# A mixer and feed-forward stack: the first chunks of a feed-forward split during the mixer before it, into tiles that its last down pairs use again

## The chip, the cores and the metric

The kernel runs on one core of a Trainium2 chip. The metric is the device time of one execution in microseconds (us), as the median of several runs; the profile is taken from one more execution of the same program.

## The reference

The input x is 256 tokens by 1024 features in float32. A first block (mixer, cross attention to a memory, mixture of experts) is not touched by the change. Then come two layers of this, each with its own weights:

```python
for l in range(2):
    x = layer_norm(alpha * x + 0.5 * swiglu(x, ffn_w_gu[l, 0], ffn_w_down[l, 0]), ...)
    mix = token_mixers(x, w_in[l], sink[l], ..., diff_subln[l], w_out[l], l)
    x = layer_norm(alpha * x + mix, ...)
    x = layer_norm(alpha * x + 0.5 * swiglu(x, ffn_w_gu[l, 1], ffn_w_down[l, 1]), ...)
```

`swiglu` is silu(x Wg) * (x Wu), times Wd, with 2816 hidden features. `token_mixers` has four attentions of four heads each (window with a sink, latent, axial, differential), whose outputs are joined and projected by `w_out`. `layer_norm` subtracts the mean, multiplies by 1/sqrt(var + eps) and by a gain, and adds a bias.

## The kernel before

Tokens lie in two tiles of 128 (t = 0, 1). Every product is made of three float32r matmuls (`mm3`, L310 to L312): the high part of one side by the high part of the other, high by low, and low by high. ACT copies the high part (`wh` of a weight, L279; `xh` of an activation, L391), and the low part is what is left after subtraction, on DVE (L392 for `xl`, L283 for `wl`).

Weights come from memory in 1 MB chunks of 128 x 2048, in the order in which they are used, by SP into a ring of four buffers (`raw`, L260); SP waits for a buffer that is free. `weight` (L265) splits a chunk into two pairs of high and low parts, 128 x 1024 each, into a ring of tiles (`wh`, `wl`, four each), or into tiles of its own (`own`, L291). The low part goes to DVE, or to POOL where `on_pool` says so: `plan` (L300) writes there, for the next chunks, whether POOL makes the low part and after which of the norm's powers it is issued.

The program is two times feed-forward, mixer, feed-forward (loop in `build`). The instructions of an engine are issued in an order that a scheduler of the framework sets from the program's dependences; `pe_order` keeps PE's order as written, and `issue_after` adds an edge of order alone.

- `ffn` (L1270): `first` takes chunks 0 and 1 (`NAT` = 2) with x as the stationary side, so that t = 0 can go ahead before x of t = 1 is there: for each t 48 matmuls of 256 columns. Then `up` chunks and `down` pairs alternate, and the last three down pairs (`TAIL` = 3) come from `own` tiles, so that the accumulators of t = 0 are finished first and its norm runs beside the matmuls of t = 1.
- `mixer2` (L1354): `mixer2_state` (L1395) makes the tiles that live through the mixer, loads and scales the sink (L1408, L1409) and `sub`, the gain of the differential attention's norm (L1415: 128 KB in pieces of 256 B; L1416: POOL multiplies it), then come projections and attentions, and at the end the output projection `dense_sq` (L341) with `ln_part` as its end. Behind it `plan("--1-")` sends the four low parts of the next feed-forward's chunks 0 and 1 to POOL, the third behind the power of t = 1.
- the norm: `ln_state` (L1241) has POOL scale the residual (`xa` = alpha x, L1247); `ln_part` (L1253) adds the product (L1261) and takes statistics (L1262); `layer_norm` (L1225) merges them (L1229), has POOL raise the variance to -1/2 (`rsqrt`, pow at L418), and makes in two halves of 512 columns (x - mean) * gain (L1234) and times 1/std plus bias (L1235, `x`). PE transposes each half (L401), ACT and DVE split it.

I call the passage from a mixer to a feed-forward seam B and the one from a feed-forward to a mixer seam A. There are two of each.

Of the kernel before, what the change touches and what calls it, by code (L numbers as in the profile page):

```python
# [12 lines left out]
AF = mybir.ActivationFunctionType  # L13
# [185 lines left out]
class Net:  # L199
    def __init__(s, ctx, tc, a, out):  # L200
        s.tc, s.nc, s.a, s.out = tc, tc.nc, a, out
        s.pos = 0
        s.on_pool = [None, None]
        s.pows, s.ahead = [], []
        s.dense_tags = ["a", "b"]
        s.nw, s.pool_mod = 0, 4
        pool = lambda n, b, **k: ctx.enter_context(tc.tile_pool(name=n, bufs=b, **k))
        s.const = pool("const", 1)
        s.ring = pool("ring", 4)
        s.xp = pool("xp", 1)  # L210
        s.st = pool("st", 4)
        s.psum = pool("psum", 1, space=bass.MemoryType.PSUM)
        nc = s.nc
        s.ident = s.const.tile([128, 128], F32, name="ident")
        s.mhalf = s.const.tile([128, 8], F32, name="mhalf")
        nc.vector.memset(s.mhalf, -0.5)
# [48 lines left out]
    def weight(s, width=CH, parts=2, pool=None, own=None, cuts=1):  # L265
# [4 lines left out]
        for i in range(parts):  # L270
# [12 lines left out]
            i = eng.tensor_tensor(l[:, :n], rc, h[:, :n].bitcast(F32), op=OP.subtract)  # L283
            if eng is s.nc.gpsimd:
                s.pool_lo = i
            if after:
# [954 lines left out]
    def ln_state(s, p, x, li):  # L1241

        g, b = s.norm_weights(p, li)
        xa = []
        for t in range(NT):
            xa.append(p.tile([128, D], F32, name=f"xa{t}"))
            i = s.nc.gpsimd.tensor_scalar(xa[t], x[t], ALPHA, None, op0=OP.mult)  # L1247
            if li == 0:
                s.issue_after(i, s.pool_lo)
        st = [s.st.tile([128, 2 + 2 * t, 6], F32, name="lnst", tag=f"lnst{t}", bufs=2) for t in range(NT)]  # L1250
        return g, b, xa, st
# [18 lines left out]
    def ffn(s, x, hs, li, last):  # L1270
        nc = s.nc
        with ExitStack() as ctx:
            p = s.pool(ctx, "ffn")
            acc = s.banks()
            hf = {}
# [24 lines left out]
            def first():  # L1300

                ps = [s.bank("mm") for _ in range(NT)]
                ws = [s.weight(cuts=1 if li else 2) for _ in range(NAT)]
                for i in range(NAT):
# [32 lines left out]
            nx = None if last else s.xsplit()  # L1337
            w = [s.weight(own=s.own(p, i)) for i in range(TAIL)]
            norm = lambda t: [s.ln_part(p, x, ln, 0.5, t, c, acc[t][c], nx) for c in range(2)]
# [10 lines left out]
            norm(1)  # L1350
            s.on_pool = []
        return nx

    def mixer2(s, x, hs, l):  # L1354
# [28 lines left out]
        with ExitStack() as ctx:  # L1383
            s.dense_tags = ["a", "b"]
            p = s.pool(ctx, "mix2o")
            ln = s.ln_state(p, x, 3 * l + 1)
            nx = s.xsplit()
            s.dense_sq(o, lambda t, c, ps: s.ln_part(p, x, ln, 1.0, t, c, ps, nx))
            s.plan("--1-")
        return nx  # L1390

    def pair(s, p, name, *shape):
        return [p.tile([128] + list(shape), F32R, name=f"{name}{i}") for i in range(2)]

    def mixer2_state(s, p, l):  # L1395

        nc = s.nc
        m = {}
        for n in ("wk", "ck"):
            m[n] = s.pair(p, n, S)  # L1400
        for n in ("wv", "cv", "mv", "dv"):
            m[n] = p.tile([128, NT, 128 if n in ("wv", "cv") else 256], F32, name=n)
        for n in ("wq", "cq", "dq", "dk"):
            m[n] = s.pair(p, n, 2, S)
        for n in ("mq", "mk"):
            m[n] = [p.tile([96, 4, S], F32R, name=f"{n}{i}") for i in range(2)]
        m["far"], m["qscale"] = s.far, s.qscale
        sink = s.bcast(p, "win_sink_2", 4, 4 * l)  # L1408
        nc.gpsimd.tensor_scalar(sink, sink, -1.0, None, op0=OP.mult)  # L1409
        m["sink"] = sink  # L1410
        lam_init = 0.8 - 0.6 * math.exp(-0.3 * l)
# [254 lines left out]
```

## Time and profile before

| what | value |
|---|---|
| median of 3 runs | 1740.98 us (1739.96 to 1743.69) |
| profiled execution: its own time | 1743.4 us |
| its span in the trace | 1741.7 us |
| mean granted TensorE clock | 0.937 |
| PE busy | 1576.9 us, 91% of the span |
| DVE busy | 840.0 us, 48% |
| ACT busy | 656.5 us, 38% |
| POOL busy | 286.5 us, 16% |
| low parts on POOL (L283) | 42, 2463 ns each |
| low parts on DVE (L283) | 314, 1249 ns each |

The engines' shares are means over stages with different limits. The mixture of experts, in the first half, waits for weights from memory; the six stages behind it fill the span from about 840 us on, and there PE is close to always busy. A wait is given with the line that waits and the instruction that ended it. The clock is the TensorE clock that was granted, as a share of 2.4 GHz.

### The profile page before, as it was taken

The page shows a single profiled execution, that of the slowest core. Times are in us where ns is not written, and L with a number is a line of the kernel's source. Part 1 is how long each engine was busy: PE and PEld are TensorE (multiplying, and loading weights), DVE is VectorE, ACT ScalarE, POOL GpSimd, SP SyncE. Part 2 cuts the span into 40 slices and gives each one's busy share as a digit, 9 for nine tenths or more (in the row PEclk, how much of TensorE's full clock was granted, in tenths as well). Part 3 has the DMA queues.
Part 4 walks back from the last instruction along what each step waited for, and adds up shares of the span by engine and source line. Part 5 has one row for each costly group of instructions (what it writes and reads, how often), then busy time and mean ns, then how long its engine had stood idle before and what let it go on. Part 6 is the DMA issues. An engine that isn't in the chain of part 4 may idle for free.

```text
span 1741.7 us, 24950 instructions
## 1 busy us (share of the span) xinstructions
PE 1576.9 (91%) x10070; PEld 1215.4 (70%) x10070; DVE 840.0 (48%) x1468; ACT 656.5 (38%) x1125; POOL 286.5 (16%) x253
## 2 busy tenths in 40 slices
PE   8998998777776776999999989999999999989998
PEld 6777774322211221799988769999999988779997
DVE  5658653000000000554577775557654677765555
ACT  4655441000000000444545645444444536734442
POOL 4224312100000000312233250000100041330000
PEclk9999998987878886999999989999999999989999
DMA  7454959999999999855543235556455634145551
GB/s 278 149 185 142 359 192 422 417 421 421 420 421 421 421 420 421 318 194 192 195 171 135 79 145 194 184 180 241 148 191 193 243 105 147 50 179 190 179 190 72
DMA packets 66187, 419.07 MB, mean 241 GB/s; under 512 B 10641, under 2 KB 12177, under 8 KB 18705
## 3 DMA queue, kind: packets, MB, share of 16 engines
q1 hardware_dynamic: 66064, 417.39, 63.2%
q8 instruction: 82, 1.34, 0.3%
q14 instruction: 41, 0.33, 0.1%
HBM read 416.32 MB, written 1.05 MB: 240 GB/s over the span
## 4 chain that ended last, share of the span: by engine, by line
PE 63%; DMA 25%; DVE 4%; issue 4%; POOL 3%; ACT 1%; SPq 0%; DVEq 0%; POOLq 0%; ACTq 0%
DMA mraw<-in_wm 23%; PE ps L310 20%; PE ps L312 19%; PE ps L311 19%; PE ps L401 2%; PE ps L480 1%; POOL wl L283 1%; DMA raw<-in_wd 1%; DVE wl L283 1%; POOL rq L418 1%; DVE xa L1234 1%; ACT wh L279 0%; DMA bc_ln_g<-in_ln_g 0%; DVE xl L392 0%; PE ps L991 0%
## 5 line engine op out<-in xcount | busy, mean ns | idle before, releaser
L283 DVE TENSOR_TENSOR wl<-raw,wh 128x1024 fp32r<-128x1024 f32 (+2 forms) x314 | 388.9, 1249 | 292.3 <-ACT wh L279 289.4
L279 ACT ACTIVATE wh<-raw 128x1024 fp32r<-128x1024 f32 (+2 forms) x356 | 370.9, 1052 | 347.3 <-PE ps L311 177.5
L310 PE MATMUL ps<-xh,wh 128*128 128x256 f32 x1424 | 402.1, 282 | 3.4 <-ACT cv L1534 3.4
L312 PE MATMUL ps<-xh,wl 128*128 128x256 f32 x1424 | 401.3, 282 | 0.0
L311 PE MATMUL ps<-xl,wh 128*128 128x256 f32 x1424 | 401.1, 282 | 0.0
L310 PEld LDWEIGHTS ps<-xh,wh 128*128 128x128 f32 x1424 | 268.3, 188 | 7.0 <-ACT cv L1534 3.8
L311 PEld LDWEIGHTS ps<-xl,wh 128*128 128x128 f32 x1424 | 268.4, 188 | 1.8 <-issue 0.4
L312 PEld LDWEIGHTS ps<-xh,wl 128*128 128x128 f32 x1424 | 268.4, 188 | 0.8
L991 PE MATMUL ps<-mraw,xg 128*32 128x512 f32 x1024 | 168.2, 763 | 70.8 <-DMA mraw<-in_wm 70.6
L312 PE MATMUL ps<-wh,xl 128*128 128x512 f32 (+3 forms) x520 | 190.2, 370 | 6.5 <-DVE xl L392 6.3
L310 PE MATMUL ps<-wh,xh 128*128 128x512 f32 (+3 forms) x520 | 190.7, 376 | 4.7 <-ACT xh L391 3.8
L311 PE MATMUL ps<-wl,xh 128*128 128x512 f32 (+3 forms) x520 | 191.9, 370 | 2.2 <-POOL wl L283 1.1
L991 PEld LDWEIGHTS ps<-mraw,xg 128*32 128x32 f32 x1024 | 26.5, 119 | 200.4 <-DMA mraw<-in_wm 164.4
L418 POOL TENSOR_TENSOR rq<-rv,mhalf 128x1 f32<-128x1 f32 (+4 forms) x46 | 46.8, 1017 | 724.6 <-DVE rv L416 721.8
L283 POOL TENSOR_TENSOR wl<-raw,wh 128x1024 fp32r<-128x1024 f32 x42 | 103.2, 2463 | 279.5 <-ACT wh L279 180.4
L997 DVE TENSOR_TENSOR mf<-ps,mf 128x512 f32<-128x512 f32 x8 | 5.5, 692 | 238.7 <-PE ps L991 234.7
L312 PEld LDWEIGHTS ps<-wh,xl 128*128 128x128 f32 x520 | 100.8, 194 | 23.3 <-DVE xl L392 10.4
L310 PEld LDWEIGHTS ps<-wh,xh 128*128 128x128 f32 x520 | 101.0, 195 | 22.1 <-ACT xh L391 7.5
L311 PEld LDWEIGHTS ps<-wl,xh 128*128 128x128 f32 x520 | 101.4, 195 | 17.9 <-POOL wl L283 3.2
L312 PE MATMUL ps<-wh,hf 128*128 128x512 f32 x256 | 100.1, 391 | 0.0
L311 PE MATMUL ps<-wl,hf 128*128 128x512 f32 x256 | 100.1, 391 | 0.0
L310 PE MATMUL ps<-wh,hf 128*128 128x512 f32 x256 | 98.2, 390 | 0.0
(351 smaller groups left out, 1965.2 us busy)
## 6 DMA issues: line engine op xcount, KB each, us to landing
mraw<-in_wm SPq DMA_DIRECT2D x191, 1024.0 KB, 19.8
raw<-in_wd SPq DMA_DIRECT2D x179, 1024.0 KB, 4.9
raw<-in_wd SPq DMA_DIRECT2D x8, 512.0 KB, 11.0
raw<-in_wd SPq DMA_DIRECT2D x4, 832.0 KB, 4.4
bc_ln_g<-in_ln_g SPq DMA_DIRECT2D x6, 512.0 KB, 5.9
bc_ln_b<-in_ln_b SPq DMA_DIRECT2D x6, 512.0 KB, 6.6
raw<-in_wd SPq DMA_DIRECT2D x4, 768.0 KB, 4.4
bias<-in_bias SPq DMA_DIRECT2D x4, 512.0 KB, 6.5
```

The costliest lines, as they stand in the source:

```text
L279: s.nc.scalar.activation(h[:, :n], rc, AF.Copy)
L283: i = eng.tensor_tensor(l[:, :n], rc, h[:, :n].bitcast(F32), op=OP.subtract)
L310: mm(out, lhsT=lh, rhs=rh, start=start, stop=False)
L311: mm(out, lhsT=lh, rhs=rl, start=False, stop=False)
L312: mm(out, lhsT=ll, rhs=rh, start=False, stop=stop)
L401: s.nc.tensor.transpose(ps[:, b * 128:b * 128 + 128], src[:, b * 128:b * 128 + 128], s.ident)
L418: s.last_pow = s.nc.gpsimd.tensor_tensor(q, r, s.mhalf[:, :n], op=OP.pow)
L480: s.nc.tensor.matmul(out, lhsT=v(j), rhs=pt[:, 2 * i + j], start=first and j == 0, stop=last and j == 1)
L991: nc.tensor.matmul(ps[32 * e:32 * e + 32], lhsT=xg[:, k, 32 * e:32 * e + 32], rhs=w[:, e * FF:e * FF + FF], start=k == 0, stop=k == NK - 1 ...
L997: nc.vector.tensor_tensor(f, gu[1], f, op=OP.mult)
L1234: nc.vector.scalar_tensor_tensor(z[:, cs], z[:, cs], mv[:, 0:1], g[:, cs], op0=OP.subtract, op1=OP.mult)
```

## The change

The names of the new file are used here; its lines stand one or a few beside those of the old one (L284 for L283, L417 for L418, L1233 and L1234 for L1234 and L1235, L1425 and L1426 for L1415 and L1416).

- A pool `front` of eight tiles (32 KB of a partition), on the right-hand side of memory, holds the split parts of chunks 0 and 1 of a feed-forward. After a mixer it is opened by `ffn_ahead`, which `dense_sq` calls before the second half of its matmuls; `first` then uses these parts. The last down pairs 0 and 1 of the same feed-forward reuse the tiles.
- `plan("--1-")` is gone, so that the low parts of chunks 0 and 1 are made by DVE.
- The residual is scaled by ACT at the feed-forwards' norms, by POOL only at the mixers'.
- `mixer2_state` makes `wk`, `wq` and the sink first, and `sub` as before behind the other tiles.

```diff
--- before.py
+++ after.py
@@ -203,6 +203,7 @@
         s.on_pool = [None, None]
         s.pows, s.ahead = [], []
         s.dense_tags = ["a", "b"]
+        s.front, s.front_parts = None, None
         s.nw, s.pool_mod = 0, 4
         pool = lambda n, b, **k: ctx.enter_context(tc.tile_pool(name=n, bufs=b, **k))
         s.const = pool("const", 1)
@@ -281,8 +282,6 @@
             after = s.on_pool.pop(0) if s.on_pool else False
             eng = s.nc.gpsimd if after is not False or (s.pool_mod and s.nw % s.pool_mod == 0) else s.nc.vector
             i = eng.tensor_tensor(l[:, :n], rc, h[:, :n].bitcast(F32), op=OP.subtract)
-            if eng is s.nc.gpsimd:
-                s.pool_lo = i
             if after:
                 s.issue_after(i, after)
             out.append((h, l))
@@ -1244,9 +1243,10 @@
         xa = []
         for t in range(NT):
             xa.append(p.tile([128, D], F32, name=f"xa{t}"))
-            i = s.nc.gpsimd.tensor_scalar(xa[t], x[t], ALPHA, None, op0=OP.mult)
-            if li == 0:
-                s.issue_after(i, s.pool_lo)
+            if li % 3 == 1:
+                s.nc.gpsimd.tensor_scalar(xa[t], x[t], ALPHA, None, op0=OP.mult)
+            else:
+                s.nc.scalar.activation(xa[t], x[t], AF.Copy, scale=ALPHA)
         st = [s.st.tile([128, 2 + 2 * t, 6], F32, name="lnst", tag=f"lnst{t}", bufs=2) for t in range(NT)]
         return g, b, xa, st
 
@@ -1271,6 +1271,10 @@
         nc = s.nc
         with ExitStack() as ctx:
             p = s.pool(ctx, "ffn")
+            if s.front is None:
+                s.front_ctx = ExitStack()
+                s.front = s.pool(s.front_ctx, "front", side="right")
+            ctx.push(s.front_ctx)
             acc = s.banks()
             hf = {}
 
@@ -1300,7 +1304,8 @@
             def first():
 
                 ps = [s.bank("mm") for _ in range(NT)]
-                ws = [s.weight(cuts=1 if li else 2) for _ in range(NAT)]
+                ws = s.front_parts or [s.weight(cuts=1 if li else 2) for _ in range(NAT)]
+                s.front_parts = None
                 for i in range(NAT):
                     hf[i] = [p.tile([128, S], F32R, name=f"hf{u}", tag=f"hf{u}", bufs=10) for u in range(2)]
                 for t in range(NT):
@@ -1335,7 +1340,7 @@
                     for c in range(2):
                         down(t, c, i, w)
             nx = None if last else s.xsplit()
-            w = [s.weight(own=s.own(p, i)) for i in range(TAIL)]
+            w = [s.weight(own=s.own(s.front if i < NAT else p, i)) for i in range(TAIL)]
             norm = lambda t: [s.ln_part(p, x, ln, 0.5, t, c, acc[t][c], nx) for c in range(2)]
             whole, lo, hi = slice(0, 512), slice(0, 256), slice(256, 512)
             with s.pe_order():
@@ -1349,6 +1354,7 @@
                             norm(0)
             norm(1)
             s.on_pool = []
+            s.front = None
         return nx
 
     def mixer2(s, x, hs, l):
@@ -1385,9 +1391,14 @@
             p = s.pool(ctx, "mix2o")
             ln = s.ln_state(p, x, 3 * l + 1)
             nx = s.xsplit()
-            s.dense_sq(o, lambda t, c, ps: s.ln_part(p, x, ln, 1.0, t, c, ps, nx))
-            s.plan("--1-")
+            s.dense_sq(o, lambda t, c, ps: s.ln_part(p, x, ln, 1.0, t, c, ps, nx), ahead=s.ffn_ahead)
         return nx
+
+    def ffn_ahead(s):
+
+        s.front_ctx = ExitStack()
+        s.front = s.pool(s.front_ctx, "front", side="right")
+        s.front_parts = [s.weight(own=s.own(s.front, i)) for i in range(NAT)]
 
     def pair(s, p, name, *shape):
         return [p.tile([128] + list(shape), F32R, name=f"{name}{i}") for i in range(2)]
@@ -1396,18 +1407,17 @@
 
         nc = s.nc
         m = {}
-        for n in ("wk", "ck"):
-            m[n] = s.pair(p, n, S)
+        m["wk"], m["wq"] = s.pair(p, "wk", S), s.pair(p, "wq", 2, S)
+        sink = m["sink"] = s.bcast(p, "win_sink_2", 4, 4 * l)
+        nc.gpsimd.tensor_scalar(sink, sink, -1.0, None, op0=OP.mult)
         for n in ("wv", "cv", "mv", "dv"):
             m[n] = p.tile([128, NT, 128 if n in ("wv", "cv") else 256], F32, name=n)
-        for n in ("wq", "cq", "dq", "dk"):
+        m["ck"] = s.pair(p, "ck", S)
+        for n in ("cq", "dq", "dk"):
             m[n] = s.pair(p, n, 2, S)
         for n in ("mq", "mk"):
             m[n] = [p.tile([96, 4, S], F32R, name=f"{n}{i}") for i in range(2)]
         m["far"], m["qscale"] = s.far, s.qscale
-        sink = s.bcast(p, "win_sink_2", 4, 4 * l)
-        nc.gpsimd.tensor_scalar(sink, sink, -1.0, None, op0=OP.mult)
-        m["sink"] = sink
         lam_init = 0.8 - 0.6 * math.exp(-0.3 * l)
         m["nlam"] = s.nlam[l]
         sub = p.tile([128, 4, 64], F32, name="sub")
```

How the order of the instructions moves is shown at three places. POOL at the first seam A, before; `own` and `wl` are the last low parts of the feed-forward, `rq` the powers (of x for t = 0 and t = 1, 128x1; of the mixer's latent norm, 128x2):

```order
L283 TENSOR_TENSOR own<-raw,own 128x1024
L283 TENSOR_TENSOR wl<-raw,wh 128x1024
L418 TENSOR_TENSOR rq<-rv,mhalf 128x1 x2
L1409 TENSOR_SCALAR bc_win_sink_6868<-bc_win_sink_6868 128x4
L418 TENSOR_TENSOR rq<-rv,mhalf 128x2
L1416 TENSOR_SCALAR sub<-sub 128x256
L1515 TENSOR_SCALAR bc_ax_q_norm_7001<-bc_ax_q_norm_7001 128x64
```

and in the changed kernel:

```order
L284 TENSOR_TENSOR own<-raw,own 128x1024
L284 TENSOR_TENSOR wl<-raw,wh 128x1024
L417 TENSOR_TENSOR rq<-rv,mhalf 128x1
L1412 TENSOR_SCALAR bc_win_sink_6856<-bc_win_sink_6856 128x4
L1426 TENSOR_SCALAR sub<-sub 128x256
L417 TENSOR_TENSOR rq<-rv,mhalf 128x1
L417 TENSOR_TENSOR rq<-rv,mhalf 128x2
L1525 TENSOR_SCALAR bc_ax_q_norm_7005<-bc_ax_q_norm_7005 128x64
```

The scaling of `sub` has moved ahead of the second power of 128x1.

SP at the same place, with the semaphores that it waits for (PE_49 counts PE's instructions), before:

```order
L260 DMA raw<-in_wd 128x1280 [waits DMAHW4_49,DVE_49]
L260 DMA raw<-in_wd 128x2048 [waits DMAHW5_49,DVE_49]
L238 DMA bc_win_sink_6868<-in_win_sink 128x4
L1415 DMA sub<-in_diff_subln 128x4x64
L1362 DMA rope<-in_rope 128x384 [waits PE_49]
L238 DMA bc_mla_q_norm_6879<-in_mla_q_norm 128x256
```

and in the changed kernel:

```order
L261 DMA raw<-in_wd 128x1280 [waits DMAHW4_49,DVE_49]
L261 DMA raw<-in_wd 128x2048 [waits DMAHW5_49,DVE_49]
L239 DMA bc_win_sink_6856<-in_win_sink 128x4
L1425 DMA sub<-in_diff_subln 128x4x64 [waits PE_49]
L1368 DMA rope<-in_rope 128x384 [waits PE_49]
L239 DMA bc_mla_q_norm_6883<-in_mla_q_norm 128x256
```

The copy of `sub` has got a wait for PE, as that of `rope` had.

DVE at the first seam B, before, from the accumulation of t = 0 (`xa_8131`; `xa_8133` is t = 1) to its x:

```order
L1261 SCALAR_TENSOR_TENSOR xa_8131<-ps,xa_8131 128x512 x2
L1262 BN_STATS lnst<-xa_8131 128x6 x2
L1229 BN_AGGR lnmv<-lnst 128x2
L416 TENSOR_SCALAR rv<-lnmv 128x1
L1234 SCALAR_TENSOR_TENSOR xa_8131<-xa_8131,lnmv,bc_ln_g_8127 128x512 x2
L1261 SCALAR_TENSOR_TENSOR xa_8133<-ps,xa_8133 128x256 x2
L1262 BN_STATS lnst<-xa_8133 128x6 x2
L1261 SCALAR_TENSOR_TENSOR xa_8133<-ps,xa_8133 128x256 x2
L1262 BN_STATS lnst<-xa_8133 128x6
L1235 SCALAR_TENSOR_TENSOR x<-xa_8131,rq,bc_ln_b_8129 128x512 x2
L1262 BN_STATS lnst<-xa_8133 128x6
L1229 BN_AGGR lnmv<-lnst 128x2
```

and in the changed kernel (`xa_8135` and `xa_8137`), from the fourth low part of the chunks 0 and 1 on, which stands behind three more of them and the accumulation of t = 0, to the gain pass of t = 0 (L1233):

```order
L284 TENSOR_TENSOR own<-raw,own 128x1024
L1262 BN_STATS lnst<-xa_8135 128x6 x2
L284 TENSOR_TENSOR wl<-raw,wh 128x1024
L1261 SCALAR_TENSOR_TENSOR xa_8137<-ps,xa_8137 128x256 x2
L284 TENSOR_TENSOR wl<-raw,wh 128x1024
L1228 BN_AGGR lnmv<-lnst 128x2
L284 TENSOR_TENSOR wl<-raw,wh 128x1024
L1261 SCALAR_TENSOR_TENSOR xa_8137<-ps,xa_8137 128x256 x2
L1262 BN_STATS lnst<-xa_8137 128x6 x2
L284 TENSOR_TENSOR wl<-raw,wh 128x1024
L415 TENSOR_SCALAR rv<-lnmv 128x1
L1233 SCALAR_TENSOR_TENSOR xa_8135<-xa_8135,lnmv,bc_ln_g_8131 128x512 x2
```

Eight low parts of 128x1024 (four `own`, four `wl` of the two chunks behind them) now stand ahead of the gain pass of t = 0; before there was none.

## Rows read from the trace of the kernel before

**Rows 1.** The list of PE's waits from 840 us to the end (total us, times, longest).

```profile
PE ps L401 <- DVE x L1235: 7.4, 2, 3.7
PE ps L312 <- DVE xl L392: 5.7, 2, 2.9
```

**Rows 2.** PE's timeline at the first seam B (start, us, line, operation, idle before).

```profile
1026.76 1.94 PE L401 MATMUL ps<-ident,x 128*128 128x128 f32 x8 [3.68 <-DVE x L1235]
1028.53 0.58 PE L310 MATMUL ps<-wh,xh 128*128 128x256 f32 x1
...
1035.04 0.39 PE L312 MATMUL ps<-wh,xl 128*128 128x256 f32 x1 [2.85 <-DVE xl L392]
```

**Rows 3.** DVE's timeline at the first seam B.

```profile
1008.58 3.62 DVE L283 TENSOR_TENSOR wl<-raw,wh 128x1024 fp32r<-128x1024 f32 x3 [0.42 <-ACT wh L279]
...
1017.51 0.69 DVE L1261 SCALAR_TENSOR_TENSOR xa<-ps,xa 128x512 f32<-128x512 f32 x1 [2.03 <-PE ps L312]
1018.12 1.28 DVE L1262 BATCH_NORM_STATS2 lnst<-xa 128x6 f32<-128x512 f32 x2
...
1019.75 3.56 DVE L1234 SCALAR_TENSOR_TENSOR xa<-xa,lnmv,bc_ln_g 128x512 f32<-128x512 f32 x2
1023.23 0.74 DVE L1261 SCALAR_TENSOR_TENSOR xa<-ps,xa 128x256 f32<-128x256 f32 x2
...
1029.12 5.26 DVE L1234 SCALAR_TENSOR_TENSOR xa<-xa,lnmv,bc_ln_g 128x512 f32<-128x512 f32 x2
1034.30 0.68 DVE L392 TENSOR_TENSOR xl<-ps,xh 128x512 fp32r<-128x512 f32 x1
```

**Rows 4.** DVE's timeline at the first seam A.

```profile
902.02 1.40 DVE L1234 SCALAR_TENSOR_TENSOR xa<-xa,lnmv,bc_ln_g 128x512 f32<-128x512 f32 x2
903.35 1.41 DVE L1235 SCALAR_TENSOR_TENSOR x<-xa,rq,bc_ln_b 128x512 f32<-128x512 f32 x2
```

**Rows 5.** POOL's timeline at the first seam B.

```profile
1020.05 2.70 POOL L283 TENSOR_TENSOR wl<-raw,wh 128x1024 fp32r<-128x1024 f32 x1 [13.25 <-ACT wh L279]
...
1028.70 5.13 POOL L283 TENSOR_TENSOR wl<-raw,wh 128x1024 fp32r<-128x1024 f32 x2
```

**Rows 6.** Stretches: PE, PEld, DVE, ACT, POOL busy; PEclk, DMA, GB/s.

```profile
1026.00:1028.00 2.00, 1.25 (x6) 1.28 (x7) 1.93 (x5) 0.12 (x1) 0.06 (x1) 0.50 0.45 98
1030.00:1032.00 2.00, 2.00 (x11) 1.89 (x9) 2.00 (x2) 0.00 (x0) 2.00 (x2) 0.50 1.01 412
1036.00:1038.00 2.00, 2.00 (x12) 2.00 (x11) 0.49 (x1) 0.00 (x0) 2.00 (x2) 0.50 0.96 406
1040.00:1042.00 2.00, 2.00 (x19) 2.00 (x18) 1.29 (x2) 1.97 (x3) 0.00 (x0) 1.00 0.00 0
```

**Rows 7.** PE's timeline at the first seam A.

```profile
904.52 1.03 PE L401 MATMUL ps<-ident,x 128*128 128x128 f32 x8
```

**Rows 8.** POOL's timeline at the first seam A.

```profile
902.19 0.98 POOL L418 TENSOR_TENSOR rq<-rv,mhalf 128x1 f32<-128x1 f32 x1 [8.30 <-DVE rv L416]
...
907.35 0.88 POOL L1416 TENSOR_SCALAR sub<-sub 128x256 f32<-128x256 f32 x1
```

**Rows 9.** SP's timeline at the first seam A (issues).

```profile
886.05 0.43 SPq L1415 DMA_DIRECT2D sub<-in_diff_subln  x1
899.72 0.34 SPq L1362 DMA_DIRECT2D rope<-in_rope  x1
```

**Rows 10.** DMA issues from 880 to 912 us (KB, us to landing).

```profile
sub<-in_diff_subln SPq DMA_DIRECT2D x1, 128.0 KB, 8.9
```

**Rows 11.** Stretches of 2 us at the first seam A, columns as above.

```profile
890.00:892.00 2.00, 2.00 (x11) 1.65 (x10) 1.02 (x2) 0.00 (x0) 0.00 (x0) 1.00 0.08 22
892.00:894.00 2.00, 2.00 (x11) 1.65 (x10) 1.93 (x5) 0.00 (x0) 1.00 (x1) 1.00 0.07 19
```

**Rows 12.** ACT's timeline at the first seam B.

```profile
1013.28 0.38 ACT L391 ACTIVATE xh<-ps 128x256 fp32r<-128x256 f32 x1 [1.20 <-PE ps L480]
1018.91 1.06 ACT L279 ACTIVATE wh<-raw 128x1024 fp32r<-128x1024 f32 x1 [5.24 <-PE ps L312]
```

## Prediction

> **What bounds the kernel now.** I read the table of engines first: PE is busy 91% of the span, so outside the MoE in the middle, which waits for its weights from memory, a change is worth what it adds to or takes from PE's waits and its clock. The list of PE's waits after 840 us then says which waits there are to gain: at the top stand two for the norm's output x and two for the low part xl, 7.4 and 5.7 us in all, two times each [rows 1]. They are the two seams from a mixer to a feed-forward (I call them B). PE's timeline shows the first: the out-projection ends at 1026.76 - 3.68 = 1023.08, PE waits 3.68 us for x, transposes it, does a few matmuls of the first chunk and waits 2.85 us more for xl until 1035.04 [rows 2]. DVE's timeline says why: the two passes that multiply by the gain take 3.56 us for t = 0 and 5.26 us for t = 1 [rows 3], where the same two passes take 1.40 us at the seam before the mixer [rows 4]. What differs is POOL, which runs its low parts over them: at 1020.05 and at 1028.70, 2.6 us each [rows 5]. The clock view adds that PE runs at half its rate (granted 0.50, the 1.2 GHz level) after the first wait and again after the second, and is back at 2.4 GHz by 1040 [rows 6].
>
> The other seam, from a feed-forward to a mixer (A), has no wait of that size in the list. PE transposes x of t = 1 at 904.52 directly behind its own work, all eight blocks in 1.03 us [rows 7], so whatever comes late there becomes a new wait. DVE wrote that x from 903.35 on [rows 4], and could do so because POOL had given the power for t = 1 at 902.19, 0.98 us long; the scaling of sub ran only at 907.35 [rows 8]. SP had issued the copy of sub at 886.05, long before, while the copy of rope waited for PE until 899.72 [rows 9].
>
> **Seam A, which the change touches without naming it.** Two orders move. The tile of sub now lies where a feed-forward's last tiles are, so its copy waits for PE, as rope's does, three matmuls earlier: 899.72 less three times 0.11 us (19 records in 2.00 us at 1040 [rows 6]) is 899.4. And on POOL the scaling of sub now stands ahead of the power for t = 1, where it stood behind two more powers. So a pow that was ready at 902.2 is queued behind a transfer. Behind the waiting POOL stand that pow, the pow of the mixer's latent norm and the axial gains; DVE's x of t = 1 waits for the first of them, and PE for that.
>
> When does sub land? The copy took 8.9 us [rows 10], but the first four of them beside weights. From 890 on it moved alone, at 22 and 19 GB/s [rows 11]: 128 KB (131,072 B) at 20.5 GB/s are 6.4 us. I take this, since in the changed kernel no weight is ahead of it; the ends are 4.9 us (from 890 to its landing at 886.05 + 8.9) and the 8.9 us of the row. It lands at 899.4 + 6.4 = 905.8. Then 0.88 for the scaling, 0.98 for the pow [rows 8], 0.18 until DVE starts (903.17 to 903.35 before) and 0.70 for half of x [rows 4]: 908.5, instead of 904.5. With 0.1 for the hop to PE the wait is **4.1 us** (2.6 to 6.6 by the ends).
>
> A wait of that length has a second price. After the wait of 3.68 us PE ran at half rate from 1026.76 to about 1032 [rows 2, 6], some 5.2 us, of which half is lost: 2.6 us. I charge **2.6** here, with 0 and 3.4 as ends (no fall; and a stretch as long as that, plus the second one's 1.7). The latent norm's pow and the copies behind sub on SP's queue follow the same delay, and by the time x of t = 1 is multiplied they are mostly there: **0.4** (0 to 1). Seam A: +7.1 each (3 to 11).
>
> The Trainium skill, "DMA: Bandwidth & Descriptors", section "Anatomy of one DMA — SWDGE (gpsimd) path", fits a copy as about 2.0 us plus its bytes over 436,000 per us, which for sub would be an estimate of 2.3 us. The 8.9 us of this trace disagree with it; by the fit seam A would cost nothing, as the second rival says.
>
> **Seam B, which the change is about.** It takes the four low parts of chunks 0 and 1 from POOL, which frees the gain passes of DVE: 3.56 to 1.40 and 5.26 to 1.40, 6.0 us less on DVE. But those four low parts stand on DVE now, and with them the four of the next two chunks, which DVE had behind the norm, and the order puts all eight ahead of the gain pass of t = 0. One low part takes 3.62 / 3 = 1.2 us [rows 3]. DVE can start when the last split of the attention is done, at 1013.28 + 0.38, and the first high part is copied, 1.06 later [rows 12]: 1014.7. From there to the first half of x of t = 0 its work is 8 x 1.2 = 9.6, two accumulations of 0.69 (1.4), statistics 1.3, four accumulations of t = 1 (2 x 0.74 = 1.5) and their statistics, about the same (1.5), small ones 0.3, the gain 1.4 and half of x 0.7 [rows 3, 4]: 17.7 us, so 1032.4. That is the wait: 1023.1 to 1032.4, **9.3 us in place of 3.68**. Then x's second half (0.7), 0.4 of small ones, the gain of t = 1 (1.4), half of x (0.7) and xl (0.68 [rows 3]) bring the first xl to about 1036.2.
>
> So at 1036.2 the changed kernel stands where the old one stood near 1035: 1.2 us later. By then the old one had done 14 matmuls of chunk 0 (the one that waits is the first to read xl of block 4: 4 blocks by three, and two) and eight transposes, the changed one only two matmuls and twelve transposes: 12 x 0.11 - 4 x 0.13 (1.03 / 8) = 0.8 to 0.9 us more. Both then run a stretch at half clock. Seam B: **+2.1** each. Ends: -2 where the single long wait costs no second half-clock stretch (1.7) and DVE starts 2 us earlier because the high parts come during the attention; +5 where the clock stays low as long as after the first wait (2.6).
>
> The Trainium skill, "SBUF — State Buffer", section "Who interferes with whom", says that a DVE instruction with two SBUF inputs contends with a GpSimd instruction that reads SBUF. The 3.56 and 5.26 us against 1.40 agree with it. By this rule alone the change would gain, as the first rival says.
>
> **The rest.** The residual scaling at the feed-forward norms goes from POOL to ACT, two copies of 1.06 us (a high part of the same size [rows 12]) right behind the first chunks, where PE waits for ACT in no large row of the list [rows 1]; its result is read only by the norm at the feed-forward's end. 0 to 0.3 each, +0.4 in all. The last tail weights reuse the shared tiles; their high parts wait for the first chunks, which are long past: 0. The reordered mixer state moves addresses and the sink's scaling: 0, apart from sub.
>
> Sum against the profiled execution of 1743.4 us (span 1741.7): 2 x 7.1 + 2 x 2.1 + 0.4 = +18.8, 1762.2. The median of the three runs, 1741.0, is 2.4 lower, so I forecast **1760 us** for the median.
>
> **Rivals.** *Faster: the norm is freed.* If DVE gets its low parts done during the attention, the gain passes cost 1.40, x of t = 0 is ready when the out-projection ends, and both waits go: 3.68 + 2.85 = 6.5 us per seam, 13 in all, 1728. For it speaks the 6.0 us that POOL takes from DVE now. Against it, that DVE has 8.4 us from 1014.7 to 1023.1 for 17.7 us of work; the first wait is shorter than now only where five or more of the eight parts lie outside that stretch, and gone with all eight; and sub must land by 901.3 at the same time (902.2 less the scaling). 0.07.
>
> *Sub lands early.* Counted back from PE at 904.5 (0.70, 0.18, 0.98 and 0.88), seam A costs nothing if sub has landed by 901.7, 2.3 us after its issue; seam B and the rest are then left, +4.6: 1748.0 beside the profile, 1745.6. For it, that no weight is on the queue any more when the copy starts, and that only the landing is seen before, not what the copy needs at least. The 20 GB/s of the copy alone speak against it [rows 11]. 0.10.
>
> *The queue is longer.* The mixer's latent norm and axial gains hang on copies behind sub and on pows behind its scaling. If these arrive later than x, a second wait of 2 to 3 us follows at 911 to 914 and the clock falls again: 11 per seam, 1768. For it: all of that comes through the two queues that the change holds up. Against it, that the copies behind sub are issued while PE waits for x anyway. 0.08.
>
> **How the numbers follow.** The forecast has 0.75 and the longer queue 0.08, both slower. A measurement of this kernel tells 0.2%, 3.5 us, from no change: the early sub, 4.6 us, lies so near it that half of its 0.10 counts as slower and half as no change. Of the freed norm's 0.07, 0.06 is faster and 0.01 inside the bound. So slower 0.88, no change 0.06, faster 0.06. The range reaches from 1746 (sub early; or A at 3 and B near -1) to 1770 (A at 11, B at 2); a freed norm and both upper ends at once are left out.
>
> **What would show it.** Right: a new wait of about 4 us, of PE's transposes for x at 905 and at the second seam A, with DVE's x waiting for POOL's pow there and POOL's sub for a DMA; SP's sub issued at about 899; a wait of about 9 us for x at 1023, gain passes of 1.4 us for two, no POOL low parts. Wrong: sub landing within 3 us of its issue; the pow of t = 1 at 902 as before; or eight low parts on DVE that run before 1014, with PE's wait at 1023 shorter than 3.7.

## The result and the profile after

The changed kernel takes 1766.1 us (median of 4 runs, 1763.8 to 1768.4) where the kernel before took 1741.0 beside it: 1.014 of it, with an interval of 1.013 to 1.015. It is slower, as forecast; the forecast was 1760, and 1766.1 lies inside its range of 1746 to 1770.

The list of PE's waits from 840 us to the end in the changed kernel (us in total, times, longest) answers to [rows 1]:

```profile
PE ps L400 <- DVE x L1234: 27.8, 4, 8.0
PE ps L309 <- ACT cv L1544: 4.0, 2, 2.0
PE ps L400 <- DVE xl L391: 2.8, 5, 1.0
```

Two waits for x have become four. PE's timeline shows one at each seam; first seam A, where [rows 7] had no wait at all, then seam B ([rows 2]):

```profile
912.36 1.94 PE L400 MATMUL ps<-ident,x 128*128 128x128 f32 x8 [6.01 <-DVE x L1234]
...
1044.07 1.94 PE L400 MATMUL ps<-ident,x 128*128 128x128 f32 x8 [8.01 <-DVE x L1234]
1047.59 1.12 PE L400 MATMUL ps<-ident,x 128*128 128x128 f32 x4 [0.95 <-DVE xl L391]
```

What x waited for at seam A stands in POOL's and SP's timelines ([rows 8] and [rows 9] before). SP:

```profile
901.04 0.38 SPq L1425 DMA_DIRECT2D sub<-in_diff_subln  x1
901.47 0.52 SPq L1368 DMA_DIRECT2D rope<-in_rope  x1
```

POOL:

```profile
910.04 0.85 POOL L1426 TENSOR_SCALAR sub<-sub 128x256 f32<-128x256 f32 x1 [14.22 <-DMA sub<-in_diff_subln]
910.86 0.57 POOL L417 TENSOR_TENSOR rq<-rv,mhalf 128x1 f32<-128x1 f32 x1
```

The copy of sub is issued 15 us later than before and takes 8.8 us (8.9 before [rows 10]); POOL stands idle for it, and the power of x of t = 1, due at 903.8, runs at 910.86. DVE's x waits for that power:

```profile
911.46 1.42 DVE L1234 SCALAR_TENSOR_TENSOR x<-xa,rq,bc_ln_b 128x512 f32<-128x512 f32 x2 [6.36 <-POOL rq L417]
```

From the list of DMA issues between 880 and 918 us (KB, us to landing), what is behind sub on the queue is late too (rope took 2.3 us before):

```profile
rope<-in_rope SPq DMA_DIRECT2D x1, 192.0 KB, 9.0
sub<-in_diff_subln SPq DMA_DIRECT2D x1, 128.0 KB, 8.8
```

In stretches of 4 us (PE, PEld, DVE, ACT, POOL busy; PEclk, DMA, GB/s) the clock falls in the wait and comes back at about 919:

```profile
908.00:912.00 4.00, 0.00 (x0) 0.00 (x0) 0.54 (x1) 0.00 (x0) 1.38 (x2) 0.54 0.33 102
912.00:916.00 4.00, 3.65 (x13) 3.18 (x14) 2.31 (x5) 2.52 (x8) 1.02 (x2) 0.50 0.05 11
916.00:920.00 4.00, 4.00 (x17) 3.77 (x17) 3.90 (x8) 2.77 (x4) 4.00 (x10) 0.68 0.26 55
```

DVE's timeline at the first seam B ([rows 3]) has the low parts ahead of the norm, and gain passes that nothing slows any more:

```profile
1027.61 3.50 DVE L284 TENSOR_TENSOR own<-raw,own 128x1024 fp32r<-128x1024 f32 x3 [0.52 <-ACT own L280]
...
1041.19 1.42 DVE L1233 SCALAR_TENSOR_TENSOR xa<-xa,lnmv,bc_ln_g 128x512 f32<-128x512 f32 x2
...
1043.17 1.41 DVE L1234 SCALAR_TENSOR_TENSOR x<-xa,rq,bc_ln_b 128x512 f32<-128x512 f32 x2
...
1044.86 1.41 DVE L1233 SCALAR_TENSOR_TENSOR xa<-xa,lnmv,bc_ln_g 128x512 f32<-128x512 f32 x2
```

**Where the 25.1 us of the span went.** I cut every trace at five marks on PE: the eight transposes of x behind the mixture of experts, the first matmul of 416 columns of a mixer, and the end of a mixer's output projection (the start of the next transposes less their wait). The parts in us, of this kernel and of those of the experiments; the time up to the first mark, 707 to 711 us, differs from run to run with the weights of the mixture of experts and is left out:

| kernel | feed-forward 1 | mixer 1 | feed-forwards 2, 3 | mixer 2 | feed-forward 4 |
|---|---|---|---|---|---|
| before | 189.4 | 123.1 | 387.7 | 123.4 | 207.5 |
| changed | 192.2 | 134.4 | 389.8 | 132.3 | 208.6 |
| sub_by_sink | 192.2 | 127.0 | 390.2 | 126.0 | 208.5 |
| sub_scale_behind | 192.3 | 127.6 | 389.9 | 125.5 | 208.6 |
| sub_short | 190.6 | 126.7 | 389.7 | 124.2 | 209.0 |
| front_left | 191.9 | 126.8 | 389.6 | 126.3 | 208.3 |
| wl_behind | 192.2 | 126.9 | 385.7 | 127.0 | 204.0 |
| left_wl | 191.9 | 123.0 | 383.7 | 125.0 | 202.6 |
| left_wl_half | 191.9 | 123.0 | 384.6 | 124.9 | 203.2 |
| left_second | 191.9 | 122.8 | 382.0 | 123.3 | 201.1 |
| before_xa_act | 191.9 | 123.0 | 387.8 | 123.4 | 207.5 |
| after_xa0 | 189.6 | 133.1 | 390.2 | 133.5 | 208.2 |
| left_second_xa0 | 189.4 | 122.9 | 382.0 | 123.3 | 201.0 |

Against the kernel before, the change lost 11.3 and 8.9 us in the mixers (seams A), 2.1 and 1.1 us in the feed-forwards behind them (seams B), and 2.8 us in the first feed-forward, where I had put nearly nothing.

Not all of the mixers' loss lies at the seam. Some way into a mixer PE waits for `cv`, the values of the axial attention, which ACT copies. Up to that wait the changed kernel takes 38.2 and 37.2 us from the mark at the first matmul of 416 columns, the kernel before 29.8 in both mixers: 8.4 and 7.4 us are lost at the seam. The wait for `cv` itself is 0.5 us longer in mixer 1 (the kernel before, then the changed one):

```profile
931.29 0.39 PE L310 MATMUL ps<-xh,wh 128*128 128x256 f32 x1 [1.51 <-ACT cv L1534]
```

```profile
941.83 0.39 PE L309 MATMUL ps<-xh,wh 128*128 128x256 f32 x1 [1.98 <-ACT cv L1544]
```

Behind it the changed kernel has, in both mixers, some 3.4 us at half the clock, which the kernel before has in neither; that is about 1.5 us more (stretches of 2 us, columns as above):

```profile
942.00:944.00 2.00, 2.00 (x12) 2.00 (x13) 1.34 (x4) 0.28 (x1) 2.00 (x7) 0.62 0.00 0
944.00:946.00 2.00, 2.00 (x12) 2.00 (x11) 1.09 (x4) 0.00 (x0) 0.63 (x3) 0.53 0.00 0
```

This does not always follow from the wait. In the traces of all thirteen kernels half the clock follows ten of the nineteen waits for `cv` of 1.9 to 2.0 us. In mixer 2 the kernel before and left_wl (below) both wait 1.88 us; one keeps the full clock (first line, from behind the wait), the other doesn't (second line):

```profile
1444.00:1446.00 2.00, 2.00 (x20) 2.00 (x19) 1.46 (x4) 0.46 (x1) 1.25 (x4) 1.00 0.00 0
```

```profile
1440.00:1442.00 2.00, 2.00 (x11) 2.00 (x11) 1.14 (x4) 0.00 (x0) 1.84 (x7) 0.50 0.01 4
```

Why it comes in one and not in the other is open. Each part in the table is from one execution, so a difference of about 1.5 us between two mixers can be such a stretch alone.

### The profile page after: what moved, and what is told of

Read it like the earlier page. It is cut to its first block, busy times and chain, and to the rows that moved or that the text cites. A ratio compares the mean times of both kernels' runs of the same rounds, so it can differ in the third digit from the quotient of the medians.

```text
span 1766.8 us, 24937 instructions
## 1 busy us (share of the span) xinstructions
PE 1587.5 (90%) x10070; PEld 1222.2 (69%) x10070; DVE 833.0 (47%) x1476; ACT 664.6 (38%) x1133; POOL 237.6 (13%) x237
## 5 line engine op out<-in xcount | busy, mean ns | idle before, releaser
L284 DVE TENSOR_TENSOR wl<-raw,wh 128x1024 fp32r<-128x1024 f32 (+2 forms) x314 | 387.4, 1243 | 302.8 <-ACT wh L280 301.3
L280 ACT ACTIVATE wh<-raw 128x1024 fp32r<-128x1024 f32 x348 | 362.3, 1052 | 349.7 <-PE ps L310 182.0
L309 PE MATMUL ps<-wh,xh 128*128 128x512 f32 (+3 forms) x456 | 170.7, 385 | 4.7 <-ACT xh L390 2.9
L310 PE MATMUL ps<-wl,xh 128*128 128x512 f32 (+3 forms) x456 | 172.3, 378 | 2.6 <-POOL wl L284 1.3
L311 PE MATMUL ps<-wh,xl 128*128 128x512 f32 (+3 forms) x456 | 170.1, 378 | 0.6 <-DVE xl L391 0.6
L417 POOL TENSOR_TENSOR rq<-rv,mhalf 128x1 f32<-128x1 f32 (+4 forms) x46 | 45.9, 998 | 779.6 <-DVE rv L415 776.9
L284 POOL TENSOR_TENSOR wl<-raw,wh 128x1024 fp32r<-128x1024 f32 x34 | 83.4, 2456 | 261.3 <-ACT wh L280 244.0
L309 PEld LDWEIGHTS ps<-wh,xh 128*128 128x128 f32 x456 | 87.4, 193 | 22.0 <-ACT xh L390 6.1
L310 PEld LDWEIGHTS ps<-wl,xh 128*128 128x128 f32 x456 | 87.7, 192 | 17.8 <-POOL wl L284 3.4
L311 PEld LDWEIGHTS ps<-wh,xl 128*128 128x128 f32 x456 | 87.1, 192 | 15.5 <-DVE xl L391 2.7
```

The lines of the kernel that those rows point to most:

```text
L280: s.nc.scalar.activation(h[:, :n], rc, AF.Copy)
L309: mm(out, lhsT=lh, rhs=rh, start=start, stop=False)
L310: mm(out, lhsT=lh, rhs=rl, start=False, stop=False)
L311: mm(out, lhsT=ll, rhs=rh, start=False, stop=stop)
L417: s.last_pow = s.nc.gpsimd.tensor_tensor(q, r, s.mhalf[:, :n], op=OP.pow)
```

## The experiments

**Seam A: sub's copy, POOL's queue, or something else?** Three runs change sub alone. The first moves its tile, so that its copy need not wait:

```diff
         nc.gpsimd.tensor_scalar(sink, sink, -1.0, None, op0=OP.mult)
+        sub = p.tile([128, 4, 64], F32, name="sub")
+        ...
+        m["sub"] = sub
         for n in ("wv", "cv", "mv", "dv"):
```

> The changed kernel with one edit: the tile of sub is made right behind the sink, so that it no longer lies where the feed-forward's last tiles are; POOL's order stays as in the changed kernel (scaling of sub ahead of the power for t = 1). Theory (sub's copy, made late by its wait for PE, holds POOL's queue): sub lands before the power is due, the two 6 us waits at the seams A and the half-clock stretches behind them go, and with them the 11.3 + 8.9 us that the two seams had grown: 1766.1 - 20.2 = 1746, between 1743 and 1749. Rival (the seam grew through the other moved tiles, or through the residual's scaling on ACT): over 1758.

Measured: 1753.9 us, 1.0064 of before (1.0047 to 1.0081), 12.2 less than the changed kernel. The waits of 6 us at the seams A are gone; PE transposes x of t = 1 without one:

```profile
905.07 1.03 PE L400 MATMUL ps<-ident,x 128*128 128x128 f32 x8
```

But the mixers keep 3.9 and 2.6 us of their loss, so the time lies between the two expectations. The theory holds for 7.4 and 6.3 us per seam; the rest has other causes. About 1.0 us in each mixer is lost at the seam: DVE makes the low part of the second half of x of t = 1 behind the latent norm's passes, at 910.12 (ahead of them before, at 908.37), and PE waits for it:

```profile
910.86 0.46 PE L311 MATMUL ps<-wh,xl 128*128 128x416 f32 x1 [0.69 <-DVE xl L391]
```

In mixer 2 the other 1.5 us are a stretch at half clock behind the wait for `cv`. In mixer 1 that wait is 0.5 us longer than before, and PE's timeline shows two short waits, the first of which the kernel before hasn't:

```profile
986.93 0.39 PE L309 MATMUL ps<-mk,mq 96*128 96x256 f32 x1 [0.74 <-ACT pr L450]
...
988.64 0.44 PE L400 MATMUL ps<-ident,pr 128*128 128x128 f32 x2 [0.51 <-DVE pr L1603]
```

Some 15 us ahead of them, at 971.28, ACT copies a weight's high part between the two exponentials of a softmax, where before it did so behind both; that the first wait comes from this was not tested. Behind the two short waits the granted clock is half for some 3.4 us in this run (two stretches, columns as above):

```profile
990.00:992.00 2.00, 2.00 (x5) 1.07 (x6) 1.30 (x5) 0.62 (x4) 0.00 (x0) 0.50 0.00 0
992.00:994.00 2.00, 2.00 (x9) 1.08 (x8) 0.00 (x0) 0.62 (x2) 0.00 (x0) 0.78 0.00 0
```

The changed kernel has the same two waits (0.74 us at 997.02, 0.51 at 998.72) and keeps the full clock behind them, and so do the other five mixers with this pair:

```profile
1000.00:1002.00 2.00, 2.00 (x11) 1.14 (x11) 1.37 (x5) 0.88 (x5) 0.00 (x0) 1.00 0.00 0
```

The second leaves the late copy and takes the scaling from POOL's way:

```diff
-        nc.gpsimd.tensor_scalar(sub, sub, 1.0 - lam_init, None, op0=OP.mult)
+        i = nc.gpsimd.tensor_scalar(sub, sub, 1.0 - lam_init, None, op0=OP.mult)
+        s.issue_after(i, s.pows[-1])
```

> The changed kernel with one edit: on POOL the scaling of sub is issued behind the power for t = 1; the copy still waits for PE and still takes its 8.8 us. Theory (POOL's queue, not the transfer, costs the time): the power comes at about 904, PE transposes x of t = 1 without a wait; only the latent norm's power stands behind sub now, at about 911, and PE needs its result at about 913: 0 to 1.5 us per seam are left, 1746 to 1751. Rival (the copies behind sub on SP's queue, landing 9 to 10 us after their issue, hold the mixer's next steps anyway): over 1756.

Measured: 1754.9 us, 1.0076 (1.0059 to 1.0093). The power runs at 903.92 and x comes on time, so POOL's queue is what made the 6 us, not the transfer by itself. PE then waits 1.67 us for the latent norm's result, whose power stands behind sub at 911.05, and 0.64 us more right after (1.33 us in the second mixer); 0 to 1.5 us were expected. Of the 4.5 and 2.1 us that the mixers keep, 3.2 and 2.0 are lost up to the wait for `cv`, so at the seam. The rest, in mixer 1, goes with the longer wait for `cv` and the short waits of the first run. Together they put the total over the expectation.

The third shortens the copy to 64 columns, 128 pieces of 256 B, which the multiplication repeats over the heads:

```diff
-        sub = p.tile([128, 4, 64], F32, name="sub")
+        sub = p.tile([128, 64], F32, name="sub")
...
-            nc.gpsimd.tensor_tensor(y3, y3, m["sub"], op=OP.mult)
+            nc.gpsimd.tensor_tensor(y3, y3, m["sub"][:, None, :].to_broadcast([128, 4, 64]), op=OP.mult)
```

> The changed kernel with one edit: sub is copied as 64 columns (128 pieces of 256 B, 32 KB) and repeated over the heads by the instruction that reads it, in place of 512 pieces (128 KB). Order and waits stay. If the landing goes with the number of pieces, sub lands about 4 us after its issue instead of 8.8, PE's waits at the seams A shrink from 6.0 to about 1.3 us and part of the half clock goes: 1749 to 1757. If the 8.8 us are the latency of such a copy whatever its size, the time stays at 1766 within 3.

Measured: 1752.1 us, 1.0058 (1.0038 to 1.0079). It lands in 3.0 us instead of 8.8 (from the list of DMA issues of this run):

```profile
sub<-in_diff_subln SPq DMA_DIRECT2D x1, 32.0 KB, 3.0
```

That is enough for the power to run at 903.46, and PE doesn't wait. So all three ways around the one wait gain about the same, 11 to 14 us.

**What is left in the mixers: the place of the shared tiles.**

```diff
-        s.front = s.pool(s.front_ctx, "front", side="right")
+        s.front = s.pool(s.front_ctx, "front")
```

> The changed kernel with one edit: the pool of the shared tiles is opened on the left-hand side of memory (ahead of the feed-forward's and the output projection's own pools), so that the mixer's long-lived tiles no longer lie under a feed-forward's last tiles. With it the orders of POOL, ACT and DVE inside the mixers are again those of the kernel before; the order at the seams B stays that of the changed kernel, with eight low parts on DVE ahead of the gain pass. Theory now (the mixers lost 11.3 and 8.9 us through the address of the shared tiles alone: some 8 by sub's late copy, and 2.6 to 3.9 more, which sub_by_sink still shows, through ACT and DVE instructions that the scheduler set in another order): the mixers take what they took before, and only the seams B's 2.1 + 1.1 us are left: 1745 (1742 to 1748). Rival (what is left of the mixers' loss belongs to the residual's scaling on ACT or to the sink's and wk's new places): as sub_by_sink, 1751 to 1755.

Measured: 1753.9 us, 1.0071 (1.0056 to 1.0087): a miss. The orders of POOL and ACT inside the mixers are as before, yet the mixers lose 3.7 and 2.9 us. SP's timeline says why: now the sink lies where something is read late, its copy waits for PE, and sub's copy is queued behind it, ahead of the others:

```profile
901.22 0.33 SPq L239 DMA_DIRECT2D bc_win_sink<-in_win_sink  x1
901.60 0.43 SPq L1425 DMA_DIRECT2D sub<-in_diff_subln  x1
902.07 0.51 SPq L1368 DMA_DIRECT2D rope<-in_rope  x1
```

Here neither the sink nor sub holds up the power of x (903.69). The copies behind sub do the harm: they land 8.6 to 11.0 us after their issue, where it was 2.3 to 4.3 before, and PE waits for the latent norm and for a low part.

```profile
914.13 0.33 PE L400 MATMUL ps<-ident,by 128*128 128x128 f32 x1 [1.36 <-DVE by L1475]
915.39 0.80 PE L310 MATMUL ps<-wl,xh 128*128 128x512 f32 x1 [0.60 <-DVE wl L284]
```

This is the rival of the longer queue, here by itself. left_wl below, where `mixer2_state` also has its old order and neither copy waits, has mixer 1 at 123.0 us, as before. Its mixer 2 takes 125.0, 1.6 more than before, which is the stretch at half clock behind the wait for `cv`.

**Seam B: which work on DVE makes PE wait?** Each of these runs changes when DVE makes low parts. The first, on top of sub_by_sink, puts the four of chunks 2 and 3 behind the norm (`xl` is the norm's last low part):

```diff
+            s.behind = [xl] * 4 if ahead else []
...
+            elif s.behind:
+                s.issue_after(i, s.behind.pop(0))
```

> sub_by_sink with one more edit: the low parts of chunks 2 and 3 of a feed-forward behind a mixer (four of the eight on DVE) are issued behind the last low part of that norm's x instead of ahead of its gain pass. Theory (DVE's queue sets the wait of PE for x at the seams B): x of t = 0 is ready 4 x 1.2 = 4.8 us earlier, the wait of 8.0 us becomes about 3.2, and 3 to 5 us per seam go against sub_by_sink: 1736 to 1741. Rival (PE needs these low parts soon after, or the wait is set by the power or the last accumulation): within 2 of sub_by_sink, with new waits of PE for these low parts.

Measured: 1745.3 us, 1.0016 (1.0006 to 1.0026). The wait went from 8.0 to 3.31 us, by 4.7 where 4.8 was worked out, and both parts with a seam B got 4.5 us shorter. The total is over the expectation by the mixers' part alone: that expectation was counted from 1746 for sub_by_sink.

> front_left with two more edits: the low parts of chunks 2 and 3 are issued behind the norm's last low part, as in wl_behind, and the mixer's state is made in the order of the kernel before (so that neither the sink nor sub waits for PE). Theory: the mixers as in the kernel before, and of the seams B what wl_behind showed between its anchors, 2.0 and 3.4 us less than before: 1741.9 - 5.4 = 1736.5 (1734 to 1739), faster than both kernels. Rival (the gain at the seams B in wl_behind was a gift of the longer mixer ahead of them): 1740 to 1743.

Measured: 1737.6 us, 0.9977 (0.9968 to 0.9986), as expected and faster than both kernels: the same four edges with the shared tiles on the left and the old order of the state.

Then, on top of left_wl, two of the four low parts of chunks 0 and 1 go to POOL:

```diff
+        s.on_pool = [None, False, None, False]
         s.front_parts = [s.weight(own=s.own(s.front, i)) for i in range(NAT)]
```

> left_wl with one more edit: of the four low parts of chunks 0 and 1, two are made by POOL and two by DVE. POOL can start them as soon as the high parts are copied, at the end of the attention, since the shared tiles need not wait for matmuls. Theory (DVE's queue ahead of the norm sets PE's wait, 3.3 us in wl_behind, and POOL is done before the gain pass): x of t = 0 is ready about 2.4 us earlier, and 1.5 to 2.5 us per seam go against left_wl: 1732 to 1735. Rival (POOL's passes slow DVE's passes of two operands beside them, as the 3.56 and 5.26 us in the kernel before showed): no gain, 1735 to 1740.

Measured: 1738.3 us, 0.9977 (0.9968 to 0.9986): no gain, the rival's case. POOL and DVE get in each other's way (POOL's timeline of this run, then DVE's):

```profile
1018.18 6.29 POOL L285 TENSOR_TENSOR own<-raw,own 128x1024 fp32r<-128x1024 f32 x2
```

```profile
1017.62 1.22 DVE L285 TENSOR_TENSOR own<-raw,own 128x1024 fp32r<-128x1024 f32 x1 [1.48 <-ACT own L281]
...
1020.14 2.05 DVE L285 TENSOR_TENSOR own<-raw,own 128x1024 fp32r<-128x1024 f32 x1
```

The low part on DVE that runs beside POOL's takes 2.05 us, the one ahead of it, over which POOL's reaches only at the end, 1.22. POOL needs 3.1 us for each, and the power of t = 0 comes behind them, at 1024.90. The scheduler also set both gain passes ahead of x, so that PE's wait rose to 5.0 us; how much of that is the order and how much the contention was not taken apart.

The last one keeps all four on DVE but puts those of chunk 1, which PE reaches only after 24 matmuls, behind the low parts of x of t = 0:

```diff
+            if ahead == s.ffn_ahead and not t:
+                s.behind = [s.last_split] * 2
+                s.front_parts.append(s.weight(own=s.own(s.front, 1)))
```

> left_wl with one more edit: the parts of chunk 1 are split behind the low parts of x of t = 0 (DVE's edge of order), so that only two of the four low parts stand ahead of the gain pass. Theory (DVE's queue sets PE's wait): from 1014.7 DVE has two low parts (2.4), then the norm of t = 0, and x is there at about 1023, when the output projection ends: the wait of 3.31 us goes to 0.5 at most, an xl of about 1 us stays, the half-clock stretch behind it gets shorter; 4 to 5 us per seam against left_wl's 1737.6: 1729 (1726 to 1732). Rival (PE meets the low parts of chunk 1 after 24 matmuls and waits there instead): 1734 to 1738, with a wait of PE for a DVE own part.

Measured: 1731.8 us, 0.9945 (0.9931 to 0.9959). PE goes from the output projection to the transposes without a wait, and what is left at the seams are waits of at most 1.2 us (from its list of PE's waits from 840 us on):

```profile
PE ps L312 <- ACT xh L396: 5.6, 9, 1.2
...
PE ps L406 <- DVE x L1240: 0.9, 2, 0.5
```

The gain against left_wl is 5.8 us by the medians, less than the 8 to 10 forecast: the wait for x went (3.3 us per seam), but several short ones for the high part of x came in its place. The clock stays full at the seams (1.00 from 1022 to 1038, where left_wl has 0.58 and 0.57 from 1026 to 1034). By the table the two seams gained 1.7 and 1.5 us against left_wl; another 1.7 us is mixer 2, where left_wl had its stretch at half clock, and that the edit did not cause.

**The residual on ACT.**

```diff
+            if li % 3 == 1:
+                s.nc.gpsimd.tensor_scalar(xa[t], x[t], ALPHA, None, op0=OP.mult)
+            else:
+                s.nc.scalar.activation(xa[t], x[t], AF.Copy, scale=ALPHA)
```

> The kernel before with one part of the change done alone: the residual is scaled by ACT at the feed-forwards' norms, by POOL only at the mixers'. Theory (a copy of 1.06 us on ACT where PE does not wait for ACT): the time of the kernel before within 1.5 us. Rival (POOL's two scalings of 5.95 us stretch DVE's passes at the seams B, so that taking them away gains): 2 to 4 us less, 1738 to 1740; or (ACT's copies hold up the split behind them): 2 to 4 us more.

Measured: 1744.9 us, 1.0020 (1.0010 to 1.0029), 3 us slower, which is the last of the rivals. In the trace four of the five parts are within 0.1 us of before and feed-forward 1 takes 2.5 us more. ACT's timeline there:

```profile
707.05 1.06 ACT L1250 ACTIVATE xa<-x 128x1024 f32<-128x1024 f32 x1 [1.94 <-DVE x L940]
708.01 1.99 ACT L279 ACTIVATE wh<-raw 128x1024 fp32r<-128x1024 f32 x2
```

The scaling stands ahead of the high parts of chunk 0, and PE waits 0.94 us for those and as long again for their low parts (before, 0.78 us for a low part alone). The clock is then 0.66 and 0.50 from 710 to 714, where before it stays at 1.00. The same edit undone in the changed kernel, at the first feed-forward alone:

> The changed kernel with one edit: at the first feed-forward (behind the mixture of experts) POOL scales the residual again, as before; at the later feed-forwards ACT still does. Theory (before_xa_act and the trace of the changed kernel: there ACT's first scaling of 1.06 us stands ahead of the high parts of chunk 0, PE then waits for them and their low parts, and the first feed-forward takes 2.5 us more): 1766.1 - 2.5 = 1763.6 (1762 to 1765). Rival (the start of the first feed-forward differs from run to run with the weights' transfers of the mixture of experts, and ACT's copies cost nothing): 1766 within 1.

Measured: 1766.8 us (1764.5 to 1767.3), a miss: the total doesn't show the 2.5 us, though in the trace feed-forward 1 is back at 189.6. Each kernel had four runs in its comparison, and their own spread is as large. With the same edit on top of left_second:

> left_second with the edit of after_xa0: the residual of the first feed-forward on POOL. Theory: another 2.5 us less than left_second, 1726.5 (1724 to 1730). Rival (as for after_xa0): the time of left_second within 1.

Measured: 1730.6 us, 0.9936 (0.9923 to 0.9950), the lowest median of all. It is 1.2 us under left_second's, where 2.5 was expected, and too little to tell the two apart; in the trace feed-forward 1 takes 189.4 us again. That the scaling costs 2.5 us in this place is shown by the traces and by before_xa_act; by the totals of the last two it is not.

## Why the prediction was right, and where it was off

The traces have 25.1 us where the sum has 18.8: the seams A came out 6.0 us higher in all, the rest 2.4 higher, the seams B 1.0 lower, and the time up to the first mark was 1.1 shorter by itself.

**Seam A, the mechanism.** It went as the working has it: sub issued late, POOL idle for it, the power behind it, PE's wait. The mark at the first matmul of 416 columns is 1.7 us later than in the trace of before, and 899.4 + 1.7 is the 901.04 that SP shows.

**Seam A, the sizes.** Forecast 7.1 us each, measured 11.3 and 8.9. The mis-sized term is the landing: I took 6.4 us from the rate of the copy alone, and it took 8.8, the upper end. The row [rows 10] had the number; that no weight was ahead in the changed kernel made no difference. With 8.8 the wait comes out at 6.5, less 0.4 for a power of 0.57 us: 6.1, against 6.01 and 5.78. Half clock lasted from the end of the wait to about 919, 6.3 us, of which half is 3.1 us (forecast 2.6). The two make 9.1 us, where the first seam lost 8.4; a wait of 0.25 us for a high part of x that the kernel before has there is gone, and the rest of that difference is not explained. The other 2.9 us of mixer 1 and 1.5 of mixer 2 come further inside: the stretch at half clock behind the wait for `cv` in both, and in mixer 1 that wait's 0.5 us and the same 0.74 us wait for an exponential as in sub_by_sink. I had put all follow-on at 0.4. The working has no term for the other orders that the scheduler gives in the middle of a mixer for a tile placed elsewhere.

The Trainium skill, "DMA: Bandwidth & Descriptors", section "Anatomy of one DMA — SWDGE (gpsimd) path", has its fit for copies issued on the gpsimd path; taken for these it would give an estimate of 2.3 us for 128 KB and 2.1 for 32 KB. Here they are issued by SP, in pieces of 256 B, and the runs show 8.8 and 3.0; the measurement decides.

**Seam B.** Forecast +2.1 each, measured +2.1 and +1.1. The wait was 8.0 us where 9.3 was worked out: the low parts began at 1027.61, 1.06 us behind the high part as counted, but low parts back to back take 3.50 / 3 = 1.17 us, statistics of t = 1 were partly left for later, and half of x came 16.3 us after that start, not 17.7. The freed gain passes did what the first rival built on, 1.42 us instead of 3.56 and 5.26 [rows 3]; it fell only because low parts took their place.

**The rest.** Forecast +0.4 in all, measured +2.8, all of it in the first feed-forward; 2.5 of it is the scaling on ACT, as before_xa_act has it alone. The step that failed: "right behind the first chunks, where PE waits for ACT in no large row of the list". That list begins at 840 us, and the first feed-forward begins at 710. The later feed-forwards cost less than 0.1, as said.

**The rivals.** The early sub did not come to pass, and sub_short shows what it would have been worth. The longer queue is real, at 3.7 and 2.9 us per mixer when alone (front_left), where it was given 4 on top. The freed norm is left_second in essence: with the low parts in the right places seams B gain 5.7 and 6.4 us each, close to the 6.5 of the two waits; the half clock behind them went too, and new short waits took some of it back.

## What to carry to other kernels

Where a change moves tiles to other addresses, read the order of every queue at the places where the old tenant is read last: a small constant's copy that has got a wait there holds whatever is behind its first reader, and the price is its whole landing time (8.8 us here), not its bytes by a rate (6.4). Work that is taken from one engine so that it no longer slows a second costs as much again if the second then does it ahead of what others wait for; splitting early pays when only the part that is needed first goes ahead. And read the waits over all the stretches that an edit touches, the first of its kind included.

## What was not expected of the hardware

- A copy of 128 KB in 512 pieces of 256 B took 8.4 to 9.7 us to land in the twelve kernels that have it, alone or beside weights; 128 such pieces (sub_short) took 3.0. All these pieces read the same 256 B, but neither that nor the bytes alone make it long: `bc_mla_q_norm`, the same 128 KB in 128 pieces of 1 KB, all from one place too, took 3.0 us in the kernel before. Whether 512 pieces from different places take as long no run shows.
- What stood behind that copy on SP's queue was late too: rope's 192 KB took 8.8 to 9.6 us there and 2.2 to 3.1 where sub had been issued long before.
- The same wait of PE is not always followed by half the clock. Ten of the nineteen waits of 1.9 to 2.0 us for `cv` were; of seven pairs of waits of 0.74 and 0.51 us within 2 us, one was (mixer 1 of sub_by_sink). Every wait of 3 to 8 us for x was.
- A low part on DVE took 2.05 us beside one on POOL and 1.22 just before, and POOL's took 3.1 us each where its others take 2.5 on average. The Trainium skill, "SBUF — State Buffer", section "Who interferes with whom", says that a DVE instruction with two SBUF inputs contends with a GpSimd instruction that reads SBUF; the trace agrees.
